# One transformer block on one core: the opening, the planner's rules for small runs, and two transpositions

## The chip, the cores and the metric

The kernel runs on one core of a Trainium2 chip. The metric is device time in microseconds (us) of one execution; lower is better. All engines run their own in-order instruction lists and wait for each other by semaphores: TensorE (PE in the rows, PEld for its weight loads), VectorE (DVE), ScalarE (ACT), GpSimd (POOL), and SyncE (SP), which issues most DMAs.

## The reference

One block for 256 tokens of width 2048, all in float32: a feed-forward (width 5632) added with weight 0.5, a mixer, and a second feed-forward, each between two RMS norms.

```python
def _rmsnorm(x, g):
    return x * rsqrt(mean(x * x, axis=-1) + 1e-6) * g
def _swiglu(x, w_gate, w_up, w_down):
    return (silu(x @ w_gate) * (x @ w_up)) @ w_down

h = x
f = _swiglu(_rmsnorm(h, ln_ffn1_pre), ffn1_gate, ffn1_up, ffn1_down)
h = h + 0.5 * _rmsnorm(f, ln_ffn1_post)
u = _rmsnorm(h, ln_mix_pre)
z_a, z_b, g_a, g_b = split(u @ w_in)              # 3360, 1024, 2048, 2048 columns
y_a = _rwkv7_branch(z_a, ...) @ w_proj_a          # a recurrence over the 256 tokens, 16 heads of 64
y_b = _pool_branch(z_b, ...) @ w_proj_b           # means over windows of 2, 4, 8, 16 tokens
h = h + _rmsnorm((sigmoid(g_a) * y_a + sigmoid(g_b) * y_b) @ w_out, ln_mix_post)
f = _swiglu(_rmsnorm(h, ln_ffn2_pre), ffn2_gate, ffn2_up, ffn2_down)
out = h + 0.5 * _rmsnorm(f, ln_ffn2_post)
```

## The kernel before

**Products.** A matrix product runs on TensorE in three matmuls per tile: each float32 operand is split into a rounded part (H, made by ScalarE as a copy to fp32r) and the rest (L, made by VectorE as a difference), and `mm3` adds H x H, H x L and L x H into a PSUM bank. Tokens are taken in two halves of 128, the inner dimension in k-tiles of 128, the columns in blocks of 512. Weights come by DMA in loads of two k-tiles (512 KB) into five buffers `w32`, and are split into five pairs `wH`, `wL`.

**Quads.** `Columns` makes two column blocks (f and l: gate and up, or two blocks of a down projection) at once. A pair of k-tiles that is a "quad" is done with seven products in place of eight, by sums of the operands (`sums`, names sf, sH, sL) and sums of the weights (names t, t13, t4), which VectorE makes. `GATE_QUADS` says how many quads each of the eleven blocks of a feed-forward has. In `block_seq` the first four products of a quad (`early`) run within the block before, the other three (`late`) within its own. The down projections use `quad` (all seven products at once); `OUT_QUADS` says for w_out how many quads there are, behind how many pairs the first comes, and how many pairs lie between them. Pairs that are quads are left out of the list `rest`, so with two quads w_out begins with k-tiles 4 and up.

**Transposed activations.** A product needs its activations with the inner dimension on the partitions. There are two ways. `transpose_split`: TensorE transposes four 128x128 tiles into a bank (tile names tr, zT, rb, pr), and the split reads the bank. `turn` and `carry`: VectorE transposes 32x32 blocks within T1 (name T), SP writes it to DRAM (name cx) and reads it back in four pieces (name x) in the wanted order, and the split reads that. The feed-forwards' hidden blocks go the second way; the norms' results and the mixer's mixed output mT go the first.

**Opening.** `head` turns 12 identity tiles (name warm), while x and the first gate column arrive; x is turned by TensorE, scaled by the gains `g1` (from a 16-row load g1rows, turned by TensorE as pg) and split; with each turned tile ScalarE sums the squares of x (name junk). Then come the 16 k-tiles of the gate column. The small parameter rows (cols) of the mixer are loaded later on SP's queue and turned by TensorE as the pair pr.

**End of a stage.** `post` evaluates the norm behind a product: for its last column block `ev` sums squares on ScalarE (junk), scales by the gains on VectorE (fg), makes the root on GpSimd (rs), and adds the residual.

**Mixer.** `MIX_ORDER` lists its products. The recurrence runs in two halves of eight heads (`rwkv`); its matmuls are small (names pA, pB, pM, pX, pU, pSa, pS, pY), use part of TensorE's rows or columns, and form the stream "chain". The results yH, yL go through w_proj_a: `pairs` does columns 0 and 1 together, k-tiles 0 to 3 of both, then 4 to 7; `gemm_tok` does columns 2 and 3 one by one. `ev_pa` multiplies by the gate sga, adds mb, and transposes into mT, which w_out reads.

**Planner.** No order is written by hand. `Plan.add` records every operation with its costs; `deadlines` works out due times, and `simulate` runs a model of the engines with a clock of its own and emits the operations in the order in which they start there. On TensorE the streams have ranks: chain, side (transpositions), main. Chain operations with the same array shape form a run (`o.run`); a run starts when `whole` finds the inputs and banks of its first 16 operations ready, and once begun goes on as its operations come free, with main matmuls in between where one is not. Two engines do not read one bank at a time (`i.lock`).

Of the kernel before, what the change touches and what calls it, by code (L numbers as in the profile page):

```python
# [19 lines left out]
P = 128  # L20
# [20 lines left out]
WARM = 12  # L41
# [4 lines left out]
GATE_QUADS = [0, 0] + [3, 4] * 4 + [3]  # L46
OUT_QUADS = ((2, 2, 1.0), (2, 1, 1.0))
# [3 lines left out]
HOLD = 3e5  # L51
Z_DMA = "k0 v0 k1 v1 r1"
# [14 lines left out]
class TileInfo:  # L67
    __slots__ = ("tag", "left", "slot", "seq", "writes", "reads", "psum", "dl", "home", "lock")
# [15 lines left out]
RUN = 16  # L84
TABLES = {AF.Exp: (0,), AF.Sigmoid: (2,), AF.Tanh: (0, 2, 18), AF.Silu: (18,)}
# [3 lines left out]
class Plan:  # L89

    def __init__(s, tc):
# [5 lines left out]
        s.clk, s.stream, s.lag, s.dl0 = 0.0, "main", 12000.0, None  # L97
# [13 lines left out]
    def tile(s, shape, dt, tag, name, pool, bufs):  # L111
        s.tags[tag] = bufs
        t = s.track(s.shadow.dram_tensor(name, tuple(shape), dt).ap(), tag)
        s.tiles[name].home = pool, list(shape), dt
        return t
# [34 lines left out]
    def add(s, eng, name, fn, a, k):  # L150
# [11 lines left out]
        s.cost(o, name, w, r, k)  # L162
        seen = set()
# [77 lines left out]
    def deadlines(s):  # L241
# [9 lines left out]
        for o in s.ops:  # L251
# [8 lines left out]
            if not run or run[-1].cfg != o.cfg or far >= idx[run[0].i]:  # L260
                run = []
# [12 lines left out]
    def simulate(s):  # L274
# [38 lines left out]
        def whole(o):  # L313
            if o.run is None or o.run is held:
                return True
            for x in o.run[:RUN]:
# [4 lines left out]
            need = {id(i) for x in o.run[:RUN] for i in x.psum if i.slot is None}  # L321
            return len(need) <= len(slots["pt"])

        def go(o):
# [144 lines left out]
class Block:  # L469
# [105 lines left out]
    def mm3(s, ps, aH, aL, bH, bL, start, stop, **k):  # L575
# [3 lines left out]
        nc.tensor.matmul(ps, aL, bH, start=False, stop=stop, **k)  # L579

    def gemm_tok(s, w, c0, at, KT, evac, lead=False, trail=False, xs=None, cw=512):
# [3 lines left out]
        def do(k, h):  # L585
            (wH, wL), (xH, xL) = ws[k], at(k)
            s.mm3(pss[h][:, :cw], xH[:, h * P:h * P + P], xL[:, h * P:h * P + P], wH, wL,
                  k == 0, k == KT - 1)
# [64 lines left out]
    def head(s, w, c0, KT, do, keep, xs):  # L653
        load, turn = xs
# [51 lines left out]
    def transpose_split(s, src, T, j, h, gT=None, stream="side"):  # L706
        nc = s.nc
        with s.set(stream=stream):
            ps = s.psum("tr").rearrange("p (k t) -> p k t", k=4)
            for i in range(4):  # L710
                nc.tensor.transpose(ps[:, i], src[:, i * P:(i + 1) * P], s.ident)
        dH = T[j][0][:, :, h * P:h * P + P]
        dL = T[j][1][:, :, h * P:h * P + P]
        if gT is not None:
# [7 lines left out]
            return  # L722
# [22 lines left out]
    def carry(s, T1, T):  # L745
        v = s.carry_raw(T1)
        T.extend(s.new_T(1))
        for h in range(2):
            H, L = [t.rearrange("p k (h i t) -> p k h i t", h=2, i=4)[:, :, h] for t in T[-1]]
# [1128 lines left out]
```

## Time and profile before

| | |
|---|---|
| median of 3 runs | 2022.7 us (2022.35 to 2023.87) |
| the profiled execution | 2022.16 us |
| its span in the trace | 2020.2 us |
| TensorE busy | 2002.1 us (99%), 9835 matmuls |
| VectorE busy | 1750.4 us (87%) |
| ScalarE busy | 1185.9 us (59%) |
| GpSimd busy | 80.7 us (4%) |
| DMA | 469.87 MB, mean 233 GB/s |
| granted TensorE clock | 0.999 |

Times in rows are us from the start of the span. A row of a timeline has its start, its length, the engine, the line of the kernel (a helper's, so it is the same for most), the operation, out<-in by the program's names, the shape and the count; in brackets the idle time of the engine before it and what ended it. Matmuls overlap in the pipeline, so a row's length is more than its share of TensorE's time; from start to start is the better measure. A row of the waits has who waited for whom, us in total, times, and the longest.

### The profile page before, as it was taken

The page shows a single profiled execution, that of the slowest core. Times are in us where ns is not written, and L with a number is a line of the kernel's source. Part 1 is how long each engine was busy: PE and PEld are TensorE (multiplying, and loading weights), DVE is VectorE, ACT ScalarE, POOL GpSimd, SP SyncE. Part 2 cuts the span into 40 slices and gives each one's busy share as a digit, 9 for nine tenths or more (in the row PEclk, how much of TensorE's full clock was granted, in tenths as well). Part 3 has the DMA queues.
Part 4 walks back from the last instruction along what each step waited for, and adds up shares of the span by engine and source line. Part 5 has one row for each costly group of instructions (what it writes and reads, how often), then busy time and mean ns, then how long its engine had stood idle before and what let it go on. Part 6 is the DMA issues. An engine that isn't in the chain of part 4 may idle for free.

```text
span 2020.2 us, 28152 instructions
## 1 busy us (share of the span) xinstructions
PE 2002.1 (99%) x9835; PEld 1652.7 (82%) x9835; DVE 1750.4 (87%) x2284; ACT 1185.9 (59%) x1592; POOL 80.7 (4%) x148
## 2 busy tenths in 40 slices
PE   9999999999999999999999999999999999999998
PEld 7888888888888888887888788888888888788886
DVE  8999999999988758897868779798999999898885
ACT  7555656565555556764846455575555665655552
POOL 0000000000001110001200110010000000000000
PEclk9999999999999999999999999999999999999999
DMA  7788888886667677756475475667888888876673
GB/s 266 239 261 268 281 268 275 266 282 219 214 203 258 214 249 206 221 162 209 143 233 179 145 261 197 200 209 241 273 273 276 269 270 273 280 227 203 208 253 133
DMA packets 254054, 469.87 MB, mean 233 GB/s; under 512 B 20559, under 2 KB 42201, under 8 KB 253913
## 3 DMA queue, kind: packets, MB, share of 16 engines
q1 hardware_dynamic: 247737, 447.63, 68.5%
q0 software_dynamic: 5888, 19.93, 2.8%
q8 instruction: 77, 1.26, 0.3%
q14 instruction: 64, 0.52, 0.1%
q10 hardware_dynamic: 288, 0.52, 0.1%
HBM read 444.40 MB, written 23.59 MB: 232 GB/s over the span
## 4 chain that ended last, share of the span: by engine, by line
PE 79%; DVE 9%; DMA 6%; issue 3%; ACT 2%; SPq 1%; DVEq 0%; ACTq 0%; POOLq 0%
PE l L455 26%; PE f L455 23%; PE mm L455 22%; PE p L455 5%; DVE wL L455 4%; DMA w<-in_ffn_gate_dram 2%; DMA x<-cx 2%; DVE t L455 1%; ACT wH L455 1%; SPq L455 1%; DMA w<-in_ffn_up_dram 1%; PE tr L455 1%; DVE w L455 0%; PE pY L455 0%; DMA x<-in_x_dram 0%
## 5 line engine op out<-in xcount | busy, mean ns | idle before, releaser
L455 ACT CAST wH<-w 128x1024 fp32r<-128x1024 f32 (+2 forms) x722 | 746.7, 1046 | 632.4 <-DVE w L455 170.8
L455 DVE TENSOR_TENSOR wL<-w,wH 128x1024 fp32r<-128x1024 f32 (+2 forms) x722 | 863.2, 1210 | 167.6 <-ACT wH L455 163.4
L455 PE MATMUL l<-wL,xH 128*128 128x512 f32 x784 | 305.7, 390 | 0.8 <-DVE wL L455 0.7
L455 PE MATMUL l<-wH,xH 128*128 128x512 f32 x784 | 305.4, 390 | 0.0
L455 PE MATMUL l<-wH,xL 128*128 128x512 f32 x784 | 305.3, 389 | 0.0
L455 PE MATMUL mm<-wL,xH 128*128 128x512 f32 (+1 forms) x672 | 261.6, 389 | 0.0
L455 PE MATMUL mm<-wH,xH 128*128 128x512 f32 (+1 forms) x672 | 261.1, 389 | 0.0
L455 PE MATMUL mm<-wH,xL 128*128 128x512 f32 (+1 forms) x672 | 260.7, 388 | 0.0
L455 PE MATMUL f<-wH,xH 128*128 128x512 f32 x664 | 258.5, 389 | 0.0
L455 PE MATMUL f<-wL,xH 128*128 128x512 f32 x664 | 258.4, 389 | 0.0
L455 PE MATMUL f<-wH,xL 128*128 128x512 f32 x664 | 258.4, 389 | 0.0
L455 DVE TENSOR_TENSOR t<-w,w 128x1024 f32<-128x1024 f32 (+1 forms) x160 | 162.1, 1013 | 14.6 <-DMA w<-in_ffn_down_dram 8.0
L455 PEld LDWEIGHTS l<-wL,xH 128*128 128x128 f32 x784 | 147.2, 188 | 32.5 <-DVE wL L455 2.2
L455 PEld LDWEIGHTS l<-wH,xH 128*128 128x128 f32 x784 | 147.2, 188 | 30.6
L455 PEld LDWEIGHTS l<-wH,xL 128*128 128x128 f32 x784 | 147.2, 188 | 30.1
L455 PEld LDWEIGHTS mm<-wL,xH 128*128 128x128 f32 x672 | 126.4, 188 | 25.2 <-DVE wL L455 0.4
L455 PEld LDWEIGHTS mm<-wH,xH 128*128 128x128 f32 x672 | 126.3, 188 | 24.9
L455 PEld LDWEIGHTS mm<-wH,xL 128*128 128x128 f32 x672 | 126.2, 188 | 24.8 <-DVE xL L455 0.4
L455 PEld LDWEIGHTS f<-wH,xH 128*128 128x128 f32 x664 | 124.6, 188 | 26.0
L455 PEld LDWEIGHTS f<-wL,xH 128*128 128x128 f32 x664 | 124.6, 188 | 25.9
L455 PEld LDWEIGHTS f<-wH,xL 128*128 128x128 f32 x664 | 124.6, 188 | 25.8
L455 DVE TENSOR_TENSOR wL<-t,wH 128x1024 fp32r<-128x1024 f32 x98 | 119.0, 1214 | 3.0 <-ACT wH L455 2.8
(307 smaller groups left out, 2697.4 us busy)
## 6 DMA issues: line engine op xcount, KB each, us to landing
w<-in_w_in_dram SPq DMA_DIRECT2D x128, 512.0 KB
w<-in_ffn_up_dram SPq DMA_DIRECT2D x114, 512.0 KB
w<-in_ffn_gate_dram SPq DMA_DIRECT2D x112, 512.0 KB
w<-in_ffn_down_dram SPq DMA_DIRECT2D x112, 512.0 KB
w<-in_ffn_gate_dram SPq DMA_DIRECT2D x190, 256.0 KB
w<-in_ffn_up_dram SPq DMA_DIRECT2D x186, 256.0 KB
w<-in_ffn_down_dram SPq DMA_DIRECT2D x128, 256.0 KB
cx<-T SPq DMA_DIRECT2D x29, 512.0 KB
```

The costliest lines, as they stand in the source:

```text
L455: ins = o.fn(*[real(x) for x in o.a], **{n: real(x) for n, x in o.k.items()})
```

## The change

- `head`: the row of gains is loaded first (with a due time far ahead) and turned before x; 16 identity turns before and 8 more behind the turn of the first two tiles of x, in a bank of the other kind; the squares of x are no longer summed with each turn but all behind k-tile 11 (`SQ`).
- `GATE_QUADS`: block 3 (the third entry) has 2 quads, not 3, in both feed-forwards.
- The planner counts TensorE's first 4.8 us of its clock double (`COLD`). Runs are cut at 16 operations and where the kind of bank changes, and `whole` asks for all of a run. In a small array shape, TensorE is left idle when the next run of the chain is ready within 400 ns (`soon`, `STAY`).
- `behind`: an operation can be put behind another in the plan. In `post`, the scaling of the last column block is put behind the step that follows its square sum.
- `ev_pa`: the blocks 0 and 1 of mT go by `turn` and `carry`; `pairs` is no longer used, and the four columns of w_proj_a run one by one. The first quad of w_out comes behind 3 pairs, not 2.

```diff
-WARM = 12
+WARM = 16
+WARM2 = 8
-GATE_QUADS = [0, 0] + [3, 4] * 4 + [3]
-OUT_QUADS = ((2, 2, 1.0), (2, 1, 1.0))
+GATE_QUADS = [0, 0, 2, 4, 3, 4, 3, 4, 3, 4, 3]
+OUT_QUADS = ((2, 3, 1.0), (2, 1, 1.0))
+MIX_DMA = 2
+COLD = 4800.0
+SQ = 11
+STAY = 400.0
...
# Plan.add
+        if s.behind is not None:
+            o.preds.add(s.behind.i)
...
# Plan.deadlines
-            if not run or run[-1].cfg != o.cfg or far >= idx[run[0].i]:
+            if not run or run[-1].cfg != o.cfg or far >= idx[run[0].i] or len(run) == RUN \
+                    or run[-1].psum[0].kind != o.psum[0].kind:
                 run = []
...
# Plan.simulate
-            for x in o.run[:RUN]:
+            for x in o.run:
...
+        def soon(o):
+            for x in o.run or [o]:
+                for q in x.preds:
+                    y = ops[q]
+                    if y.eng != "PE" and (y.start is None or y.end + 305.0 > now + STAY):
+                        return False
+            need = {id(i) for x in o.run or [o] for i in x.psum if i.slot is None}
+            return len(need) <= len(slots["pt"])
...
+            if e == "PE" and now < COLD:
+                pace, dur = 2 * pace, dur + pace
...
+                            if q and st == "chain" and cfg != (0, 0) and can(q[0]) and soon(q[0]):
+                                break
...
# head
-        ps = s.psum("warm")
+        ps = s.bank("warm")
         for _ in range(WARM):
             s.nc.tensor.transpose(ps[:, :P], s.ident, s.ident)
+        load(None, None)
         load(0, 0)
         load(1, 0)
-        load(None, None)
...
-        turn(1, 0)
+        last = turn(1, 0)
         split(2)
         split(3)
+        with s.set(behind=last):
+            for _ in range(WARM2):
+                s.nc.tensor.transpose(ps[:, :P], s.ident, s.ident)
         for k in range(KT):
             do(k, 0)
-            do(k, 1)
+            last = do(k, 1)
...
+            if k == SQ:
+                late = last
+        with s.set(behind=late):
+            for c in range(4):
+                for h in range(2):
+                    square(h, c)
...
# post, last column block
                     s.sumsq(ps, ss[h][:, c:c + 1])
-                    norm(h, r)
-                    scale()
+                    with s.set(behind=norm(h, r)):
+                        scale()
...
# mixer, ev_pa
-                s.transpose_split(sg, mT, c, h)
+                if c >= MIX_DMA:
+                    s.transpose_split(sg, mT, c, h)
+                    return
+                if not h:
+                    T1.append(s.unit(p="T1"))
+                s.turn(T1[0], h, sg)
+                if h:
+                    s.carry(T1[0], mT, c)
...
-        s.pairs(prm["w_proj_a"], (0, 512), at_a, NKW, 4, (ev_pa(0), ev_pa(1)))
-        for c in range(2, 4):
+        for c in range(4):
             s.gemm_tok(prm["w_proj_a"], c * 512, at_a, NKW, ev_pa(c))
...
# tile_block_kernel, load(None, None)
-                nc.sync.dma_start(out=gr, in_=ln_ffn1_pre[0].rearrange("(k p) -> k p", p=P))
+                with s.set(lag=-20000.0):
+                    nc.sync.dma_start(out=gr, in_=ln_ffn1_pre[0].rearrange("(k p) -> k p", p=P))
```

More of the change, by code (lines that the diff above doesn't have):

```diff
@@ L67 @@
 class TileInfo:
-    __slots__ = ("tag", "left", "slot", "seq", "writes", "reads", "psum", "dl", "home", "lock")
+    __slots__ = ("tag", "left", "slot", "seq", "writes", "reads", "psum", "dl", "home", "lock", "kind")
 class Engine:
@@ L114, in tile @@
         s.tiles[name].home = pool, list(shape), dt
+        s.tiles[name].kind = name.rsplit("_", 1)[0]
         return t
@@ L578, in mm3 @@
         nc.tensor.matmul(ps, aH, bL, start=False, stop=False, **k)
-        nc.tensor.matmul(ps, aL, bH, start=False, stop=stop, **k)
+        return nc.tensor.matmul(ps, aL, bH, start=False, stop=stop, **k)
     def gemm_tok(s, w, c0, at, KT, evac, lead=False, trail=False, xs=None, cw=512):
@@ L653, in head @@
     def head(s, w, c0, KT, do, keep, xs):
-        load, turn = xs
+        load, turn, square = xs
         w32 = {}
@@ L710, in transpose_split @@
             for i in range(4):
-                nc.tensor.transpose(ps[:, i], src[:, i * P:(i + 1) * P], s.ident)
+                last = nc.tensor.transpose(ps[:, i], src[:, i * P:(i + 1) * P], s.ident)
         dH = T[j][0][:, :, h * P:h * P + P]
@@ L1111, in emit @@
                     s.rstd(ss[h], D, rs[h])
-        return uT, rs, emit
+        def emit(h, c, ap):
+            s.transpose_split(ap, uT, c, h, gT())
+            square(h, c, ap)
+        return uT, rs, emit, square
     def tok(s, w, c0, at, KT, evac):
@@ L1373, in ev_pa @@
         def ev_pa(c):
+            T1 = []
             def ev(h, ps):
@@ L1795 @@
         g1 = s.const([P, 16], "g1")
-        uT, rs, pre = s.next_pre(lambda: g1)
+        uT, rs, _, square = s.next_pre(lambda: g1)
         nc = s.nc
```

35 lines of the change are left out of this document (19 added, 16 removed).

## The prediction

> **What bounds the kernel now.** I read the page first, then the waits of TensorE, then the chain of waits, then the timeline at the places that the change touches: the opening, the small matmuls of the recurrence, the end of the mixer, the end of the kernel.
>
> ```profile
> span 2020.2 us, 28152 instructions
> ...
> PE 2002.1 (99%) x9835; PEld 1652.7 (82%) x9835; DVE 1750.4 (87%) x2284; ACT 1185.9 (59%) x1592; POOL 80.7 (4%) x148
> ```
>
> TensorE (PE) is busy 2002.1 of 2020.2 us. The time is therefore the length of its instruction list, plus its few waits, plus what lies before its first and after its last instruction. An edit pays if it shortens that list or one of these waits, and an edit that relieves VectorE (87%) or ScalarE (59%) pays only through a wait of TensorE. From the waits of TensorE, the three that the change could reach outside the recurrence (total us, times, longest):
>
> ```profile
> PE l L455 <- DVE hL L455: 1.5, 2, 1.2
> PE pr L455 <- DMA cols<-in_pool_scale_dram: 1.2, 1, 1.2
> ...
> PE l L455 <- DVE wL L455: 0.7, 1, 0.7
> ```
>
> The profiled execution took 2022.16 us, 2.0 more than its span; the median of the three runs is 2022.7, 0.54 above it. The sum below is made against 2022.16, and 0.54 is added at its end. About 0.2% (4.05 us) is what a measurement of this kernel tells from no change.
>
> **Part 1: one quad less in each feed-forward.** The third entry of GATE_QUADS goes from 3 to 2. A quad does seven products (four in `early`, three in `late`) where plain pairs of k-tiles do eight (2 k-tiles, 2 halves, 2 columns); a product is three matmuls. From the chain of waits, start, us and what:
>
> ```profile
> 1259.87 16.32 PE l L455 x72
> ```
>
> 16.32 / 72 = 0.227 us per matmul back to back. So 3 x 0.227 = 0.68 us more in each of the two feed-forwards, **+1.36 us**, all on TensorE. VectorE is relieved of a quad's additions and splits; at most this ends the waits for hL and wL shown above (2.2 us), but the trace has those waits in later blocks, so I count nothing; the range keeps both ends.
>
> **Part 2: two blocks of the mixer's output by VectorE.** For columns 0 and 1 the four groups of four transpositions leave TensorE. The timeline shows two such groups between matmuls:
>
> ```profile
> 1204.77 0.60 PE L455 MATMUL tr<-ident,sga 128*128 128x128 f32 x4
> 1205.12 0.48 PE L455 MATMUL mm<-wH,yL 128*128 128x512 f32 x1
> 1205.45 0.60 PE L455 MATMUL tr<-ident,sga 128*128 128x128 f32 x4
> ...
> 1206.12 0.39 PE L455 MATMUL mm<-wL,yH 128*128 128x512 f32 x1
> ```
>
> From 1204.77 to 1206.12 are 1.35 us with two matmuls of 0.227 in them, so 0.90 for two groups, 0.45 each (the slower matmul behind a group included). Four groups: **-1.79 us**. What they cost elsewhere must be hidden: VectorE's transposition, a write to DRAM, four reads, the splits. The same route is in the feed-forward, and the rows around the mixer's end give the room:
>
> ```profile
> 57.56 1.29 DVE L455 STREAM_TRANSPOSE T<-sg 128x512 f32<-128x512 f32 x2
> ...
> 69.38 1.14 ACT L455 CAST xH<-x 128x512 fp32r<-128x512 f32 x2 [0.84 <-DMA x<-cx]
> ```
> ```profile
> 1184.20 0.68 DVE L455 TENSOR_TENSOR yL<-qb,yH 128x512 fp32r<-128x512 f32 x1
> ...
> 1186.63 0.39 PE L455 MATMUL mm<-wH,yH 128*128 128x512 f32 x1
> ...
> 1232.94 0.39 PE L455 MATMUL f<-wH,xH 128*128 128x512 f32 x1
> ```
>
> The product with w_proj_a begins at 1186.63. A column is 8 k-tiles x 2 halves x 3 matmuls x 0.227 = 10.9 us, so column 1 ends at 1208.4 when the columns run one after the other. VectorE then has four operations on 128x512 (0.68 each by the yL row) and 1.29 of transposition, 4.0 us; from there to the first split of the landed tile pass 10.5 us (58.85 to 69.38), and splitting takes some 2.5: ready near 1225.4. w_out starts with k-tiles 4 to 7, which are column 1, near 1231 (1186.63 + 43.5 + 0.9 of remaining groups). Some 5.6 us to spare, so nothing is added. The new DMAs go on SP's queue between the loads of w_out; what is queued behind them are those loads. The first quad of w_out moves one pair later (OUT_QUADS), which gives column 0 time and changes no count: 0. Without `pairs`, k-tile 4 of the first column is needed at 1186.63 + 24 x 0.227 = 1192.1, before it was 5.4 us later; yL is done at 1184.9. 7.2 us to spare: 0.
>
> A rule of the Trainium skill speaks against this part: VectorE: DVE Perf Modes, Rules for kernel authors, says to transpose a full 128x128 on TensorE if PSUM is an acceptable destination. By it the four groups stay and the sum would be 1.79 us higher. I keep the rows, because TensorE is the engine with no idle time here and VectorE has some.
>
> **Part 3: last square first.** At the very end:
>
> ```profile
> 2011.14 0.69 DVE L455 TENSOR_TENSOR fg<-l,gb 128x512 f32<-128x512 f32 x1 [5.74 <-PE l L455]
> 2011.87 0.60 ACT L455 ACTIVATE junk<-l 128x512 bf16<-128x512 f32 x1 [10.19 <-DVE fg L455]
> ...
> 2012.59 0.21 DVE L455 TENSOR_SCALAR rt<-ss,rp 128x1 f32<-128x1 f32 x1 [0.75 <-ACT junk L455]
> ...
> 2013.53 2.74 DVE L455 SCALAR_TENSOR_TENSOR fg<-fg,rs,h 128x512 f32<-128x512 f32 x4 [0.73 <-POOL rs L455]
> ```
>
> The square waits 0.73 us for the scaling. With `behind` the square comes first and the scaling runs while GpSimd takes the power: 0.73 us of VectorE's idle time before 2013.53 holds its 0.69. Nothing else is late there: **-0.73 us**. At the ends of the first feed-forward and the mixer TensorE has other matmuls: 0.
>
> **Part 4: the opening.** TensorE's first rows, VectorE's first two and ScalarE's first scaled one:
>
> ```profile
> 1.71 2.82 PE L455 MATMUL warm<-ident 128*128 128x128 f32 x12 [1.71 <-POOL ident masks.py:199]
> 5.28 1.97 PE L455 MATMUL tr<-ident,x 128*128 128x128 f32 x8 [0.75 <-DMA x<-in_x_dram]
> 7.18 0.28 PE L455 MATMUL pg<-ident,g1rows 16*128 16x16 f32 x1
> ...
> 8.17 0.78 PE L455 MATMUL mm<-wH,xH 128*128 128x512 f32 x1
> ...
> 28.34 0.39 PE L455 MATMUL mm<-wL,xH 128*128 128x512 f32 x1
> 29.95 0.53 PE L455 MATMUL pr<-ident,cols 128*128 128x128 f32 x2 [1.22 <-DMA cols<-in_pool_scale_dram]
> ```
> ```profile
> 6.52 0.69 DVE L455 TENSOR_TENSOR wL<-w,wH 128x512 fp32r<-128x512 f32 x1 [6.52 <-ACT wH L455]
> 7.50 0.17 DVE L455 COPY g<-pg 128x16 f32<-128x16 f32 x1 [0.29 <-PE pg L455]
> ```
> ```profile
> 7.71 0.88 ACT L455 ACTIVATE xH<-tr,g 128x128 fp32r<-128x128 f32 x3
> ```
>
> The first product waits for the gains (7.18, 7.50, 7.71, then 8.17), although x is turned and the first weights are split by 7.21. With the row first, about 1 us of this goes. But the stretch ends at 29.95, where TensorE waits 1.22 us for small rows queued behind x (2 MB), the gate's first column (4 MB) and five loads of the up column (2.5 MB); those transfers do not change. A faster opening alone only lengthens that wait. The gain is the number of matmuls that the planner places ahead of the pr pair: it puts the pair where its own clock has the rows landed, and its matmuls begin earlier by about the 0.7 us that pass from 7.50 to 8.17, so 3 more come first: **-0.68 us**. Bounds: 0 and -1.22. The eight extra turns cost 8 x 2.82 / 12 = 1.9 us ahead of the first product at worst, most of it in idle time; up to 0.54 (1.22 - 0.68) more is covered by the same wait. The squares, moved from between the turns to behind k-tile 11, lie on ScalarE; what waits for them are rs, the Silu and the sums for the next quads, which `GATE_QUADS` also asks for later: 0.
>
> **Part 5: whole runs.** In the recurrence a run of pA and pB is now at most 16 operations of one kind of bank, and starts when all of it can. Now they are broken up (first half), while the first pA goes through whole:
>
> ```profile
> 866.73 0.39 PE L455 MATMUL mm<-wH,xH 128*128 128x512 f32 x1
> 867.05 2.05 PE L455 MATMUL pA<-AR,BK 64*128 64x128 f32 x32
> 869.04 0.50 PE L455 MATMUL mm<-wL,xH 128*128 128x512 f32 x1
> ...
> 882.10 0.24 PE L455 MATMUL pB<-ident,BK 64*128 64x64 f32 x1 [0.30 <-ACT X L455]
> 882.27 0.51 PE L455 MATMUL mm<-wH,xL 128*128 128x512 f32 x1
> 882.71 0.70 PE L455 MATMUL pB<-ident,BK 64*128 64x64 f32 x15
> ...
> 888.51 0.39 PE L455 MATMUL mm<-wL,xH 128*128 128x512 f32 x1
> 888.83 0.72 PE L455 MATMUL pB<-ident,BK 64*128 64x64 f32 x16
> 889.48 0.50 PE L455 MATMUL mm<-wH,xL 128*128 128x512 f32 x1
> ```
>
> A whole pA costs 869.04 - 866.73 - 0.23 = 2.08 us, a whole pB 889.48 - 888.51 - 0.23 = 0.74, and the matmul behind each takes 0.11 more than usual (0.50 against 0.39). The stretches by window, large matmuls (mm) alone; one of each count began before and one at the end:
>
> ```profile
> 881.41:889.48 8.07, 3.55 (x12) 1.00 0.54 165
> 1077.89:1084.13 6.24, 2.83 (x10) 1.00 0.01 3
> ```
>
> First half: 8.07 - 10 x 0.227 = 5.80 for two pB and one pA, which whole would be 2 x 0.74 + 2.08 + 0.22 = 3.78: 2.0 too many. Second half: 6.24 - 8 x 0.227 = 4.42 for one pB and one pA, whole 0.74 + 2.08 + 0.11 = 2.93: 1.5. Of these 3.5 us about 1 is waiting on ScalarE and VectorE, which can come back; I take **-2.8 us**, bounds 0 and -3.5. STAY lets TensorE idle up to 400 ns in place of going back to large matmuls; no row shows it, and I take 0 between -0.5 and +0.5.
>
> Sum: 1.36 - 1.79 - 0.73 - 0.68 - 2.80 = -4.64. 2022.16 - 4.64 = 2017.5, and 0.54 more is **2018.0 us**.
>
> **The rivals.** (a) The gains of parts 4 and 5 do not come: the pr pair keeps its place, and the runs, which the planner cuts by its estimates, still break on the chip's real waits. Then 2018.0 + 0.7 + 2.8 = 2021.5. For it: the breaks have waits in them (0.30 before 882.10). Against it: the rule acts on the order itself. (b) The plan is redrawn everywhere, and the waits for hL and wL (2.2 us) and the rest of the pr wait (0.5) go too: 2015.3. For it: they are single waits with no pattern. Against it: nothing in the change is aimed at them. (c) Slower: a whole run waits for all its banks, so the recurrence ends later, and w_proj_a's k-tile 4 now comes earlier. Place: the second half, before 1192.1. From a delay of 7.2 us on, each us is one of TensorE's waiting, since w_proj_a is next in its order. In the first half pB began 13 us after pA had ended (869.04 to 882.10); a hold of that size for both pB and the second pA would end the recurrence some 17 us later, a wait of 10: 2028. Against it: the matmuls that fill the hold exist, and yL has its 7.2 us. (d) The rule of the skill holds: the route takes twice its 10.5 us beside w_out's loads, column 1 is ready at 1235.9, 4.9 after 1231, so 2022.9.
>
> **How the numbers follow.** Forecast 0.57, (a) 0.17, (b) 0.13, (c) 0.08, (d) 0.05. The forecast's own range is 2016.2 (part 4 at -1.22, part 5 at -3.5, STAY at -0.5) to 2020.3 (half of part 5, 0.4 of part 4 lost, STAY at +0.5); 0.40 of its 0.57 I put beyond 4.05 us (below 2018.65) and 0.17 within. Faster: 0.40 + 0.13 = 0.53. Same: 0.17 + 0.17 + 0.05 = 0.39. Slower: 0.08. The range 2014.8 to 2022.3 takes in the forecast, (a) and nearly all of (b).
>
> **What would show it.** Right: TensorE's matmul count six large ones higher; transpositions of sga x16 instead of x32, with two more writes of cx and eight more reads; junk ahead of fg at the end and the last gap 0.7 shorter; pB in groups of 16 and pA of 32; the wait of pr about half as long. Wrong: a wait of f or mm for xL or yL after 1186, pr's wait longer than 1.2, or new waits of l for wL in the first 140 us, which would mean that late squares starve the sums.

## The result and the profile after

The changed kernel takes 2033.3 us (median of 10 runs, 2028.6 to 2038.7) where the kernel before, on the same chip, takes 2022.7 (10 runs, 2021.0 to 2026.2): a ratio of 1.0052, 95% interval 1.0040 to 1.0064, so 10.5 us slower. Forecast were 2018.0 us and a range of 2014.8 to 2022.3; the time lies 11 us above the range. The profiled execution took 2032.80 us, its span is 2031.1. All readings below are of profiled executions; differences between kernels that were measured in runs are given as ratios to the kernel before, which ran beside them each time (its median there was 2023.8 to 2025.0); a thousandth of the ratio is 2.0 us. The code stands on other lines now: what was L455 is L477 in the changed kernel, and between L455 and L479 in the others.

The page of the changed kernel, and the waits of its TensorE (total us, times, longest):

```profile
span 2031.1 us, 28147 instructions
...
PE 2002.6 (99%) x9837; PEld 1655.5 (82%) x9837; DVE 1744.9 (86%) x2278; ACT 1185.6 (58%) x1588; POOL 80.9 (4%) x148
```
```profile
PE tr L477 <- DVE sga L477: 8.5, 1, 8.5
PE pS L477 <- ACT Z L477: 2.9, 1, 2.9
...
PE tr L477 <- DMA x<-in_x_dram: 1.7, 1, 1.7
PE l L477 <- DVE hL L477: 1.4, 2, 1.2
PE pk L477 <- DVE nb L477: 1.2, 1, 1.2
...
PE pr L477 <- DMA cols<-in_pool_scale_dram: 0.5, 1, 0.5
```

TensorE is as busy as before (2002.6 against 2002.1 us). It has two matmuls more than before: six large ones more by part 1, twelve more turns of the identity by part 4, and sixteen transpositions fewer by part 2. The span grew by 10.9, and one line carries most of it: a transposition of sga waits 8.5 us for VectorE, a wait that the kernel before does not have. Its place in the timelines of TensorE, ScalarE, VectorE and GpSimd (start, us, what, and in brackets the idle time before it and who ended it):

```profile
1223.57 0.39 PE L477 MATMUL mm<-wH,yL 128*128 128x512 f32 x1
1232.42 1.09 PE L477 MATMUL tr<-ident,sga 128*128 128x128 f32 x4 [8.47 <-DVE sga L477]
1233.16 0.78 PE L477 MATMUL mm<-wH,yH 128*128 128x512 f32 x1
...
1236.29 0.63 PE L477 MATMUL mm<-wH,yL 128*128 128x512 f32 x1
...
1237.11 0.39 PE L477 MATMUL mm<-wL,yH 128*128 128x512 f32 x1
```
```profile
1214.52 1.05 ACT L477 CAST wH<-w 128x1024 fp32r<-128x1024 f32 x1 [2.39 <-DMA w<-in_w_proj_a_dram]
1223.53 1.14 ACT L477 CAST xH<-x 128x512 fp32r<-128x512 f32 x2 [7.96 <-DMA x<-cx]
1224.58 2.93 ACT L477 CAST wH<-w 128x1024 fp32r<-128x1024 f32 x3
```
```profile
1202.15 1.30 DVE L477 STREAM_TRANSPOSE T<-sga 128x512 f32<-128x512 f32 x2
...
1224.18 1.29 DVE L477 TENSOR_TENSOR xL<-x,xH 128x512 fp32r<-128x512 f32 x2 [8.80 <-ACT xH L477]
1225.40 2.35 DVE L477 TENSOR_TENSOR wL<-w,wH 128x1024 fp32r<-128x1024 f32 x2
...
1230.40 1.28 DVE L477 TENSOR_TENSOR sga<-mm,sga 128x512 f32<-128x512 f32 x2
```
```profile
1189.68 0.53 POOL L477 DMA_DIRECT2D h<-hsp  x1 [11.80 <-PE mm L477]
1202.64 0.53 POOL L477 DMA_DIRECT2D h<-hsp  x1 [12.42 <-DVE sga L477]
1203.85 0.53 POOL L477 DMA_DIRECT2D h<-hsp  x1 [0.69 <-DVE T L477]
1209.56 0.53 POOL L477 DMA_DIRECT2D h<-hsp  x1 [5.18 <-ACT wH L477]
```

Read from the end: TensorE's transposition of column 2 needs sga, which VectorE makes at 1230.40. It makes it late because it stood idle for 8.80 us, up to 1224.18, waiting for xH. ScalarE made that late because it stood idle for 7.96 us, up to 1223.53, waiting for column 0 to come back through cx. Nothing on TensorE needs column 0 then. But each engine works its list off in order, and the split of column 0 stands in both lists ahead of the weight casts and of column 2's evacuation. Column 0 had been transposed at 1203.45, so 20.1 us passed up to the split, where the feed-forward's route, by the prediction's rows, takes 10.5. In these 20 us three of the four loads of h and one of gb (512 KB each, issued by GpSimd) run beside the write and the reads of cx and the weight loads: between 1203 and 1224 GpSimd's queue moves 2.10 MB and SP's 3.83. The time goes into the reads and not into the write. They are issued by 1211.16, and 12.4 us pass from there to the split:

```profile
1208.99 2.17 SPq L477 DMA_DIRECT2D x<-cx  x4
```

The wait has a sequel. Busy time of TensorE and its granted clock (PEclk) in stretches of 4 us:

```profile
core 0: us, PE busy (x), PEclk, DMA share, GB/s
1224.00:1228.00 4.00, 0.00 (x0) 0.85 0.31 116
1228.00:1232.00 4.00, 0.00 (x0) 0.50 0.87 255
1232.00:1236.00 4.00, 3.58 (x13) 0.50 0.98 291
1236.00:1240.00 4.00, 4.00 (x17) 0.87 0.45 143
```

The clock falls to half during the wait and stays there until about 1237: from 1233.16 to 1237.11 pass 3.95 us with seven large matmuls and a group of transpositions, which at the prediction's durations take 7 x 0.227 + 0.45 = 2.04. With the slow group at 1232.42 that is some 2.2 us more. The Trainium skill, TensorE: Matmul & The Clock Gate, What's actually happening, says that an idle window of about 3.4 us halves the clock and about 3.4 us of sustained work restore it; by that rule a wait of 8.5 us is followed by slow matmuls, and the trace agrees.

The whole difference by position: counting all matmuls of 256 columns and more, number 5132 starts at 1223.31 us before and 1222.89 after (0.4 earlier), number 5142 at 1226.14 and 1236.72: 11.0 us are lost between them. The last one starts 11.7 us later, of which six more products are 1.36; the end of the kernel behind it takes 8.64 in place of 9.52.

### The profile page after: what moved, and what is told of

Its sections match the earlier page's. It is cut to its first block, busy times and chain, and to the rows that moved or that the text cites. A ratio compares the mean times of both kernels' runs of the same rounds, so it can differ in the third digit from the quotient of the medians.

```text
span 2031.1 us, 28147 instructions
## 1 busy us (share of the span) xinstructions
PE 2002.6 (99%) x9837; PEld 1655.5 (82%) x9837; DVE 1744.9 (86%) x2278; ACT 1185.6 (58%) x1588; POOL 80.9 (4%) x148
## 4 chain that ended last, share of the span: by engine, by line
PE 68%; DVE 13%; DMA 8%; issue 5%; ACT 4%; SPq 1%; DVEq 0%; POOL 0%; ACTq 0%; POOLq 0%
PE l L477 23%; PE f L477 20%; PE mm L477 18%; DVE wL L477 6%; PE p L477 5%; DMA x<-cx 3%; DMA w<-in_ffn_gate_dram 3%; ACT wH L477 2%; DVE t L477 2%; SPq L477 1%; DMA w<-in_ffn_up_dram 1%; DVE w L477 1%; DMA w<-in_w_proj_a_dram 1%; DVE T L477 1%; PE tr L477 0%
## 5 line engine op out<-in xcount | busy, mean ns | idle before, releaser
L477 ACT CAST wH<-w 128x1024 fp32r<-128x1024 f32 (+2 forms) x722 | 748.2, 1047 | 625.9 <-PE mm L477 142.8
L477 DVE TENSOR_TENSOR wL<-w,wH 128x1024 fp32r<-128x1024 f32 (+2 forms) x722 | 864.6, 1211 | 162.3 <-ACT wH L477 158.5
L477 PE MATMUL l<-wL,xH 128*128 128x512 f32 x788 | 307.1, 390 | 0.0
L477 PE MATMUL l<-wH,xH 128*128 128x512 f32 x788 | 306.9, 389 | 0.0
L477 PE MATMUL l<-wH,xL 128*128 128x512 f32 x788 | 306.6, 389 | 0.0
L477 PE MATMUL f<-wL,xH 128*128 128x512 f32 x672 | 261.7, 389 | 0.2 <-DVE wL L477 0.2
L477 PE MATMUL f<-wH,xL 128*128 128x512 f32 x672 | 261.6, 389 | 0.0
L477 PE MATMUL f<-wH,xH 128*128 128x512 f32 x672 | 261.4, 389 | 0.0
L477 PE MATMUL mm<-wH,xH 128*128 128x512 f32 (+1 forms) x672 | 261.0, 388 | 0.0
L477 PE MATMUL mm<-wH,xL 128*128 128x512 f32 (+1 forms) x672 | 260.9, 388 | 0.0
L477 PE MATMUL mm<-wL,xH 128*128 128x512 f32 (+1 forms) x672 | 260.6, 388 | 0.1
L477 PEld LDWEIGHTS l<-wL,xH 128*128 128x128 f32 x788 | 147.9, 188 | 31.5 <-DVE wL L477 0.7
L477 PEld LDWEIGHTS l<-wH,xH 128*128 128x128 f32 x788 | 147.9, 188 | 30.6
L477 PEld LDWEIGHTS l<-wH,xL 128*128 128x128 f32 x788 | 147.9, 188 | 30.2
L477 DVE TENSOR_TENSOR t<-w,w 128x1024 f32<-128x1024 f32 (+1 forms) x156 | 158.5, 1016 | 16.1 <-DMA w<-in_ffn_down_dram 8.3
L477 PEld LDWEIGHTS f<-wL,xH 128*128 128x128 f32 x672 | 126.1, 188 | 27.0 <-DVE wL L477 0.7
L477 PEld LDWEIGHTS f<-wH,xH 128*128 128x128 f32 x672 | 126.2, 188 | 26.1
L477 PEld LDWEIGHTS f<-wH,xL 128*128 128x128 f32 x672 | 126.2, 188 | 26.1
L477 PEld LDWEIGHTS mm<-wH,xL 128*128 128x128 f32 x672 | 126.2, 188 | 25.0
L477 PEld LDWEIGHTS mm<-wL,xH 128*128 128x128 f32 x672 | 126.2, 188 | 25.0 <-DVE wL L477 0.5
L477 PEld LDWEIGHTS mm<-wH,xH 128*128 128x128 f32 x672 | 126.2, 188 | 24.5
L477 DVE TENSOR_TENSOR wL<-t,wH 128x1024 fp32r<-128x1024 f32 x96 | 116.8, 1217 | 5.5 <-ACT wH L477 5.1
```

The source lines that it names most:

```text
L477: ins = o.fn(*[real(x) for x in o.a], **{n: real(x) for n, x in o.k.items()})
```

## The experiments

**Four runs on the wait: without the route, the route alone, later splits, later reloads.**

```diff
# e1_no_route, against the changed kernel
-MIX_DMA = 2
+MIX_DMA = 0
```

> The changed kernel with MIX_DMA = 0: all four columns of the mixer's output are transposed by TensorE again, the rest of the change stays. Theory (the route makes the wait of 8.5 us for sga at the end of the mixer, and the slow matmuls behind it): the wait and the slow matmuls (2.2 us) go and four groups of four transpositions come back (+1.8), so 2033.3 - 8.5 - 2.2 + 1.8 = 2024.4 us. Rival (the wait is the doing of the new order of the recurrence, and only shows at this place): a wait of over 4 us stays near 1223 and the time stays above 2030. If moreover the opening and the whole runs bring what the prediction gave them, the time is 2018.0 + 1.8 = 2019.8.

Measured: 2024.02 us, 0.9995 of before (0.9983 to 1.0007). The list of TensorE's waits has none for sga any more, and the clock stays at 1.00 from 1224 to 1240. The reloads by GpSimd are early again, the last of the four before 1191:

```profile
1185.22 0.53 POOL L477 DMA_DIRECT2D h<-hsp  x1 [7.37 <-ACT wH L477]
1188.17 0.53 POOL L477 DMA_DIRECT2D h<-hsp  x1 [2.43 <-DVE qb L477]
1189.42 1.12 POOL L477 DMA_DIRECT2D h<-hsp  x2 [0.72 <-PE mm L477]
```

So part 2 carries the whole loss, and parts 1, 3, 4 and 5 together bring about 1 us (by the interval, from 3.4 us gained to 1.4 lost) where the prediction had 2.85.

```diff
# e2_route_only, against the kernel before
-OUT_QUADS = ((2, 2, 1.0), (2, 1, 1.0))
+OUT_QUADS = ((2, 3, 1.0), (2, 1, 1.0))
+MIX_DMA = 2
...  # carry(s, T1, T, j=None) and ev_pa as in the change
-        s.pairs(prm["w_proj_a"], (0, 512), at_a, NKW, 4, (ev_pa(0), ev_pa(1)))
-        for c in range(2, 4):
+        for c in range(4):
```

> The kernel before with part 2 alone: MIX_DMA = 2, the four columns of w_proj_a one after the other, and the first quad of w_out one pair later. Theory (the route alone is enough): a wait of 6 to 9 us for sga near 1225 and slow matmuls behind it, 2022.7 - 1.8 + 8.5 + 2.2 = 2031.6 us. Rival (it takes the new order of the recurrence too, which delays the tiles that the reloads wait for): no wait over 2 us there, 2022.7 - 1.8 = 2020.9.

Measured: 2036.57 us, 1.0053 of before (1.0034 to 1.0072). The route alone is enough:

```profile
PE tr L456 <- DVE sga L456: 9.0, 1, 9.0
```

The h loads are issued at 1187.88, 1201.01, 1202.22 and 1207.36, as in the changed kernel, so it is the route that moves them: its tiles T1 and x32 come from the same 34 units as h, and the loads wait for units that the route holds or that come free later (the second and third row of GpSimd above wait for sga and for T). That the units are the reason is read from these rows; no run gave the route units of its own.

```diff
# e3_late_split, against the changed kernel
-                o.end = dma + LAND
+                o.end = dma + LAND + o.far
...
-                    s.carry(T1[0], mT, c)
+                    with s.set(far=5000.0):
+                        s.carry(T1[0], mT, c)
```

> The changed kernel in which the planner counts 5 us more for each of the two steps (write, read back) of the two mixer blocks, so that their splits stand behind more weight casts in the lists of ScalarE and VectorE; no instruction is added. Theory (the splits stand too early in lists that are worked off in order, and what waits for them is the work behind them): the wait for sga falls below 2 us, and with it the slow matmuls; 2033.3 - 8.5 - 2.2 = 2022.6 us or a little more. Rival (the blocks themselves come too late for w_out, or the weights of w_out do): a wait of mm for xL, xH, wH or wL of 4 us or more takes its place, and the time stays above 2029.

Measured: 2029.32 us, 1.0020 of before (1.0011 to 1.0029). TensorE's waits at the place:

```profile
1239.78 1.48 PE L479 MATMUL tr<-ident,sga 128*128 128x128 f32 x8 [2.72 <-DVE sga L479]
...
1242.58 0.80 PE L479 MATMUL f<-wH,xH 128*128 128x512 f32 x1 [1.31 <-ACT xH L479]
...
1244.20 0.80 PE L479 MATMUL f<-wH,xL 128*128 128x512 f32 x1 [0.40 <-DVE xL L479]
```

Neither side comes out in full: the wait for sga is 2.7 us and not under 2, and the rival's time comes (above 2029) without its wait of 4 us. Moving the splits behind more of the casts takes 5.8 us off the first wait, so the order of the lists does carry the price. But the transfer is as slow as ever (22.4 us from the end of the transposition at 1206.80 to the split at 1229.21, still with 2.46 us of idle ScalarE ahead of it), and now w_out does wait for a block, 1.7 us, at half clock. Order alone cannot mend a transfer that takes twice its time.

```diff
# e4_reload_late, against the changed kernel
+        o.sem = s.behind if o.nbytes else None
...
+                if o.sem is not None:   # a real wait, not only one in the plan
+                    s.tc.add_manual_dep(ins.ins, did[o.sem.i].ins.name, info, reason="slot")
...
                 if h == 0:
-                    reload()
+                    with s.set(behind=s.last):   # the last transposition of sga by TensorE
+                        reload()
```

> The changed kernel with the four loads of h from hsp (2 MB, by GpSimd) held until the last transposition of the mixer's output by TensorE, so that they no longer lie in the same time as the write and the reads of cx. Theory A (they compete with the transfers of cx for the DMA engines): from the transposition of column 0 to its split passes 12 us or less in place of 20, the wait for sga falls below 2 us, 2033.3 - 10.7 = 2022.6 us. Theory B (the queue of weight loads on SP alone makes the transfer that slow): 17 us or more, and a wait of 5 us or more stays: above 2028.

Measured: 2022.50 us, 0.9985 of before (0.9975 to 0.9995): some 13.6 us faster than the changed kernel by the two ratios, with the same work, and faster than the kernel before.

```profile
1238.55 2.25 POOL L478 DMA_DIRECT2D h<-hsp  x4 [60.36 <-PE f L478]
```
```profile
1215.91 1.14 ACT L478 CAST xH<-x 128x512 fp32r<-128x512 f32 x2 [0.75 <-DMA x<-cx]
```
```profile
1208.74 1.84 SPq L478 DMA_DIRECT2D x<-cx  x4
```

With the loads of h held until 1238.55 (and with them the load of gb, which stands behind them in GpSimd's list), column 0 is transposed at 1203.76 (end) and split at 1215.91: 12.2 us in place of 20.1, at the edge of what theory A asked for. From the end of the issue of the reads (1210.58) to the split pass 5.3 us in place of 12.4, so 7 of the 8 us are lost in the reads; from the issue of the write to that of the reads it is 4.9 (from 1203.84) in place of 5.5 (from 1203.53). ScalarE waits 0.75 for it, TensorE 0.5 for sga, and its clock stays at 1.00. So the wait of 8.5 us rests on two things, the transfer slowed by GpSimd's loads and a split that stands early in lists worked off in order; taking the first away leaves 0.5 us of it, taking the second away 2.7. The Trainium skill, DMA: Bandwidth & Descriptors, Issuing engines are not separate DMA queues, says that transfers issued by GpSimd and by SP run on the same 16 DMA engines and interleave; the trace agrees, since loads on another engine's queue lengthen SP's round trip from 12.2 to 20.1 us.

**The other parts alone.** Four runs on whole runs (part 5) and on the quad (part 1), all but the first on top of the held reloads:

```diff
# e5_runs_only, against the kernel before: part 5 alone
-            if not run or run[-1].cfg != o.cfg or far >= idx[run[0].i]:
+            if not run or run[-1].cfg != o.cfg or far >= idx[run[0].i] or len(run) == RUN \
+                    or run[-1].psum[0].kind != o.psum[0].kind:
...  # whole over the run, soon and STAY as in the change
```

> The kernel before with part 5 alone (runs of one kind of bank, at most 16, started whole, and STAY). Theory P (the prediction's step): broken runs become whole at no other cost, -2.8 us, a ratio to before of 0.9986. Theory N (read from the profiles with part 5, which all show a wait of pk for nb of 1.2 us and mostly a wait of pS for Z of over 2.5, where those without it show 0 and 0.9 to 1.4): the runs become whole, and these two waits, some 3 us, take the gain back; a ratio of 1.000 within 0.001, and both waits in the profile. If the two waits are missing here, they come from another part.

```diff
# e6_late_old_quads, against e4_reload_late
-GATE_QUADS = [0, 0, 2, 4, 3, 4, 3, 4, 3, 4, 3]
+GATE_QUADS = [0, 0] + [3, 4] * 4 + [3]
# e7_late_no_runs, against e4_reload_late: the lines of e5 undone
# e8_late_no_runs_old_quads: both
```

> The kernel with the held reloads (e4_reload_late) with GATE_QUADS as before the change: one quad more in each feed-forward. By the count of matmuls (6 x 0.227) it is 1.36 us faster than that one: 0.9985 - 0.0007 = 0.9978 of before. Rival (the quad left out relieved VectorE of waits that come back): waits of l for hL and wL of over 1.4 us more in the sum, and no gain, 0.9985 or more.

> The kernel with the held reloads (e4_reload_late) without part 5, so with the rule of before for runs. Theory P: 2.8 us slower than that one, 0.9999 of before. Theory N: no slower than 0.5 us, perhaps 1 faster, 0.998 to 0.9988; the wait of pk for nb is gone and that of pS for Z is under 1.5.

> Both at once: held reloads, GATE_QUADS and the rule for runs as before the change; what stays of the change is the route, the last square and the opening. By sums: -1.8 (route) - 0.75 (square) - 0.1 (opening, as the profiles show it) = -2.65 us against before, a ratio of 0.9987. With theory N the one with the old quads and part 5 comes out alike, within 0.7 us; with theory P that one is 2.8 faster.

Measured: e5 2025.70 us, 1.0002 of before (0.9991 to 1.0012); e6 2023.86 us, 0.9995 (0.9985 to 1.0005); e7 2022.18 us, 0.9985 (0.9977 to 0.9994); e8 2025.33 us, 1.0000 (0.9990 to 1.0011). Part 5 brings nothing that can be measured, alone (e5) or beside the rest (e7 against e4): theory N, except that the wait of pS is not its doing, since e7 without it still has 2.5 us. With the old quads the kernel is slower, not faster, by 2.0 us (e6 against e4) and 3.0 (e8 against e7) by the ratios, each uncertain by almost 3 us as worked out from the two intervals: the sum that predicted -1.36 seems to have missed an interaction, which the next runs look for.

**The opening and the quad.**

```diff
# e9_head_only, against the kernel before: part 4 alone (head, load, square and COLD as in the change)
# e10_head_and_quads, against e9_head_only
-GATE_QUADS = [0, 0] + [3, 4] * 4 + [3]
+GATE_QUADS = [0, 0, 2, 4, 3, 4, 3, 4, 3, 4, 3]
# e11_quad_first_only, against e7_late_no_runs
-                              su, [2 * i for i in range(GATE_QUADS[b])],
+                              su, [2 * i for i in range(GATE_QUADS[b] + (b == 2 and xs is None))],
# e12_no_head, against e8_late_no_runs_old_quads: the opening as in the kernel before
```

> The kernel before with part 4 alone (row of gains first, more turns of the identity, square sums from k-tile 11). Prediction's step: -0.68 us, a ratio of 0.9997. Theory S (read from e6 and e8, where the late squares put the Silu of block 0 some 3 us later and the sums of the first quads with it): the pr pair stays at 30.0 to 30.1 with one matmul more ahead, and a wait of l for wH and wL of 1.3 to 1.6 us appears near 79; +1.3 us, a ratio of 1.0006.

> The kernel before with parts 4 and 1 (the opening, and 2 quads in block 3). Theory S: the wait near 79 is gone, since there is a quad less to prepare, and six matmuls more come instead, +1.36 - 0.1: a ratio of 1.0006, the same as with part 4 alone within 1 us. Rival (the quad left out relieves more than this wait, as the medians of e4 against e6 and of e7 against e8 would have it, 2.0 and 3.1 us): 0.9995 or less, faster than part 4 alone by 2 us or more.

> The kernel with held reloads and without part 5 (e7_late_no_runs) with the quad left out in the first feed-forward alone; the second has its three quads in block 3 again. Theory S (the quad left out pays only where the late squares are): 3 matmuls less, -0.68 us, 0.9982 of before. Rival (it relieves VectorE in both): not faster than e7_late_no_runs, 0.9985 or more, and waits of l for hL or wL of over 0.7 near 1390.

> What the other runs leave as paying, alone: the kernel before with the route of part 2, the last square first, and the reloads held; opening, quads and runs as before the change. By sums: -1.8 - 0.75 + 0.5 (wait for sga that the held reloads leave) = -2.0 us, 0.9990. With theory S it is 1.3 us or more faster than e8_late_no_runs_old_quads, which has the new opening too (1.0000).

Measured: e9 2027.83 us, 1.0018 (1.0009 to 1.0026); e10 2025.91 us, 1.0006 (0.9997 to 1.0015); e11 2022.89 us, 0.9989 (0.9980 to 0.9998); e12 2023.74 us, 0.9994 (0.9984 to 1.0004). Part 4 alone costs 3.6 us, more than theory S has. Its wait near 79 us, on TensorE, and on ScalarE the Silu of block 0 that stands at its root (e9, and below it the same Silu in a kernel with the early squares, e13_quads_only):

```profile
78.52 0.39 PE L463 MATMUL f<-wH,xL 128*128 128x512 f32 x1
79.60 0.50 PE L463 MATMUL l<-wH,xH 128*128 128x512 f32 x1 [0.70 <-ACT wH L463]
80.86 0.50 PE L463 MATMUL l<-wL,xH 128*128 128x512 f32 x1 [0.76 <-DVE wL L463]
```
```profile
39.68 1.27 ACT L463 ACTIVATE sg<-mm,rs 128x512 f32<-128x512 f32 x2
```
```profile
35.97 0.69 ACT L455 ACTIVATE sg<-mm,rs 128x512 f32<-128x512 f32 x1
37.49 0.69 ACT L455 ACTIVATE sg<-mm,rs 128x512 f32<-128x512 f32 x1
```

The squares from k-tile 11 on put the scales rs, and with them the Silu, about 3 us later; what VectorE prepares for the quads moves with it, and TensorE waits 1.46 us. The same two waits are in e6 (1.3 us) and e8 (1.6 us), which have late squares and three quads, and, at this place, in no profile with two quads or with early squares. Two quads in block 3 leave VectorE the time: e10 has no such wait, and S's ratio, though it is 2.4 us faster than e9 where S had less than 1.

How much of this lies in the opening can be read by position. The 400th large matmul (512 columns) starts at 103.8 to 104.2 us in the seven profiles with the old opening, at 105.9 to 106.2 in the three with late squares and three quads, and at 104.3 to 104.7 in the seven with late squares and two. So the late squares cost about 2 us there; the quad left out takes back 1.5 of them, at a price of 0.68 for three more matmuls in each feed-forward, and 0.5 stays. The rest of e9's loss arises later.

e11 gives back the quad in the second feed-forward, where there are no late squares, and does not get the 0.68 us that theory S gives it (0.9989 against 0.9985; the intervals are wider than the difference, so this stays open).

**Part 1 alone, and without the opening.**

```diff
# e13_quads_only, against the kernel before
-GATE_QUADS = [0, 0] + [3, 4] * 4 + [3]
+GATE_QUADS = [0, 0, 2, 4, 3, 4, 3, 4, 3, 4, 3]
# e14_late_quads_no_head: e12_no_head with this line
# e15_late_quads_runs_no_head: e14 with part 5
```

> The kernel before with part 1 alone (2 quads in block 3 of each feed-forward). Prediction's step, and theory S (a quad less pays only where the late squares are): six matmuls more, +1.36 us, 1.0007. Rival R (it relieves VectorE of work by which TensorE waits in many places for hL and wL): 0.9993 or less, waits of l of 1.0 us or less in the sum, where the kernel before has 2.2.

> The kernel before with the route of part 2, held reloads, the last square first and part 1, so e7_late_no_runs (0.9985) with the opening of before. Theory S: e12_no_head + 1.36 us, 1.0001. Rival R: e12_no_head - 2 to 3 us, 0.9980 to 0.9984, and then faster than any kernel so far, if the opening costs anything.

> The same with part 5 as well, so the held reloads (e4_reload_late, 0.9985) with the opening of before: within 1 us of e14_late_quads_no_head, since part 5 by itself came out at 1.0002 and at no difference between e4 and e7. If the opening of part 4 costs 1 to 3 us, it is faster than e4_reload_late by that: 0.997 to 0.998.

Measured: e13 2026.76 us, 1.0012 (1.0003 to 1.0020); e14 2023.58 us, 0.9993 (0.9984 to 1.0002); e15 2021.95 us, 0.9994 (0.9985 to 1.0003). e13 is 2.4 us slower, with the sign of the prediction, and rival R's time does not come. But the profile does not put that loss where a quad is missing: e13 is 0.8 us behind the kernel before when the first feed-forward is done (first transposition of fg), 7.5 at the first product of w_proj_a and 6.2 at the end, so most of it arises in the mixer, which part 1 does not touch. R's other sign, waits of l of 1.0 us or less, does come (0.3), but these waits are between 0.2 and 4.4 us in the seventeen profiles, with two quads and with three, so it tells nothing. e14 lies between the two theories, and e15 does not reach the 0.997 to 0.998 expected of it.

By the ratios the opening, which alone costs 3.6 us, gains 1.2 to 1.8 where the quad is out (e10 against e13, e7 against e14, e4 against e15). Each of these differences is uncertain by some 2.5 us and taken from kernels on different chips, and at the 400th matmul the kernels with the new opening are 0.5 us later, not earlier. So that it gains there is not shown. What is shown of parts 1 and 4 together is the wait of 1.5 us that the one makes and the other takes away. The lowest ratios are those of e4_reload_late and e7_late_no_runs, both 0.9985 with intervals below 1: the first is the whole change with the reloads held, the second the same without part 5.

## Why the prediction was wrong, point by point

**Part 2, the step that failed.** "Some 5.6 us to spare, so nothing is added" was wrong in its time and in its victim. The time was the feed-forward's 10.5 us from transposition to split, taken over to a place where other loads run; it measured 20.1 (20.6 in e2, 22.4 in e3), and 12.2 with GpSimd's loads away. The prediction did look at the queue, but only at SP's ("what is queued behind them are those loads"); the loads that did the harm are GpSimd's, and the route brought them to this place (e1, e2), by our reading because it takes units that they need. The kernel before issues them between 1181.54 and 1186.98, over 16 us before the route's write (1203.53), so its trace had no row of the collision. The victim was taken to be w_out, which needs the blocks at 1231. It was column 2's evacuation, which needs no block at all and only stands behind the splits in the lists of VectorE and ScalarE. The question of who is queued behind the waiting instruction was put for SP and not for these two. Then the slow clock added some 2.2 us to 8.5, so the term that was put at nothing measured 10.7. The transpositions saved are real: from the first product of w_proj_a to the first of w_out pass 46.31 us in the kernel before and 44.47 in e7, which has the route and waits less than 0.2 us in this stretch; 1.84 less, against 1.79 in the sum.

Rival (d) came nearest, with 5 in 100: it had the transfer at twice its time, but let the loss begin only where w_out needs column 1, and so got 4.9 us. The rule of the Trainium skill to transpose on TensorE (VectorE: DVE Perf Modes, Rules for kernel authors) would have been the better choice for the change as it stands (by the two ratios e1 is some 11 us faster), but not for a reason in the transposition: VectorE's took 1.30 us for two, as in the feed-forward.

**Part 1** has its six matmuls, and e13 (+2.4, from 0.6 to 4.0) does not speak against their +1.36, though most of e13's loss lies elsewhere. It was wrong in being summed: with part 4's late squares it takes away a wait of 1.5 us.

**Part 3** was right. The end of the changed kernel, ScalarE and VectorE:

```profile
2022.83 0.60 ACT L477 ACTIVATE junk<-l 128x512 bf16<-128x512 f32 x1 [10.19 <-PE l L477]
```
```profile
2023.55 0.21 DVE L477 TENSOR_SCALAR rt<-ss,rp 128x1 f32<-128x1 f32 x1 [7.18 <-ACT junk L477]
2023.68 0.68 DVE L477 TENSOR_TENSOR fg<-l,gb 128x512 f32<-128x512 f32 x1
2024.49 2.74 DVE L477 SCALAR_TENSOR_TENSOR fg<-fg,rs,h 128x512 f32<-128x512 f32 x4
```

The square (junk) now comes ahead of fg, whose 0.68 lies in the time of GpSimd's power. From the start of the last matmul to the end of the span pass 8.64 us (9.52 before): 0.9 less, against 0.73. In the eleven profiles with part 3 it is 8.6 to 8.9 us, in the six without 9.4 to 10.1.

**Part 4** had the mechanism and missed the size and the price. The matmuls that were to begin 0.7 us earlier begin where x lands; the first product begins at 8.74 here, and at 7.4 to 8.3 in the other nine kernels with the new opening, against 8.17 before:

```profile
7.46 0.66 PE L477 MATMUL tr<-ident,x 128*128 128x128 f32 x4 [1.68 <-DMA x<-in_x_dram]
...
8.74 0.48 PE L477 MATMUL mm<-wH,xH 128*128 128x512 f32 x1
...
30.09 0.53 PE L477 MATMUL pr<-ident,cols 128*128 128x128 f32 x2 [0.55 <-DMA cols<-in_pool_scale_dram]
```

As foreseen, the pr pair holds the stretch (30.09, before 29.95), but one matmul more comes ahead of it and not three: the 101st large product starts at 35.3 to 35.6 us in ten profiles with the new opening and at 35.6 to 36.1 in seven with the old, 0.3 us on average against 0.68. The squares, counted at nothing because the quads were asked for later, cost about 2 us at the 400th matmul where the quad was not left out, 1.5 of them in the wait, and 0.5 where it was.

**Part 5** did what was said of the order and brought less. Runs of the recurrence in the changed kernel:

```profile
882.05 1.07 PE L477 MATMUL pB<-ident,BK 64*128 64x64 f32 x16
885.34 2.06 PE L477 MATMUL pA<-AR,BK 64*128 64x128 f32 x32
...
1076.45 2.05 PE L477 MATMUL pA<-AR,BK 64*128 64x128 f32 x30 [0.23 <-DVE AR L477]
...
1083.54 0.68 PE L477 MATMUL pB<-ident,BK 64*128 64x64 f32 x15 [0.30 <-DVE AR L477]
```

They start whole, in four pieces of each half, but then wait inside: the rule acts on the planner's estimate of when an operand is there. From the starts of the matmuls on both sides, the four runs of the first half cost 6.30 us in place of 7.64 and those of the second 7.10 in place of 7.24; with 0.11 for each matmul behind a break that is gone (two and two) that is 1.6 and 0.4 us, where 2.0 and 1.5 were said. And the wait of pk for nb, 1.2 us, is in all seven profiles with part 5 and in none of the ten without. What is left, 0.8 us, is less than the runs can tell (e5: -1.8 to +2.4). Rival (c) did not come: yL is done 5.2 us later than before (1190.09 against 1184.88), within the 7.2 to spare, and no product waits for it.

The sum, by what the runs show: part 2 +10.7 (e2, net of the transpositions saved, 6.9 to 14.6), parts 1 and 4 together +1.2 (e10), part 3 -0.9, part 5 about 0: +11.0, against the measured 10.5. The terms from runs are uncertain by 2 to 4 us each, so that the sum comes out this well is luck. In the profiles, 8.9 of the 10.8 us between the two spans arise between the first product of w_proj_a and the first of w_out (8.5 + 2.2 - 1.8).

## What to carry to other kernels

A round trip through DRAM has no price of its own: take its time from a row in which the same loads run beside it, and ask which transfers, of every issuing engine, the change itself will move into that time by taking their buffers. Where engines work lists off in order, an early place in a list makes a late operand everyone's wait: ask for each engine that handles it what stands behind, not only who needs the result. Edits that move work of one engine (late squares) and edits that relieve it (a quad less) are measured together as well as alone.

## What was not expected of the hardware

TensorE's clock also fell in waits far shorter than 8.5 us. The wait of pS for Z, near 950 us, is 0.9 us in the kernel before and between 1.3 and 3.5 in the sixteen others, with no pattern by part. Up to 1.4 us (three profiles) the clock stays at 1.00 behind it. From 2.0 to 3.5 us it falls to 0.50 in ten of fourteen, for 3.4 us in eight and 6.8 in two, and not in four (waits of 2.0, 2.1, 2.6 and 3.0). So the length of the wait alone does not decide, and by our estimate (half of the time at 0.50) such a wait may cost up to 1.7 or 3.4 us more than its own time. The Trainium skill, TensorE: Matmul & The Clock Gate, What's actually happening, has idle windows of about 3.4 us that run free of the kernel; here a wait of 2.0 us was enough.

Near 834 us the clock falls to 0.50 for 3.4 us in six profiles (e3, e8, e9, e12, e13, e14), in four of them with no wait of more than 0.2 us in the 8 us ahead. What stands there are sixteen very small matmuls. In e9 (the second row has the stretch, its length, TensorE's busy time and matmuls, its clock, the DMA share and GB/s):

```profile
831.72 1.95 PE L463 MATMUL pn<-bones,sq 128*128 128x2 f32 x16
```
```profile
834.00:836.00 2.00, 2.00 (x13) 0.60 0.03 11
```

TensorE is busy in all of this stretch, at a mean clock of 0.60. The other eleven profiles have the same sixteen matmuls and no fall. What decides stays open.

The falls also come and go between executions of one kernel: the kernel before has none near 834 or 950 in its profile, and its executions in the runs have mean clocks of 0.996 to 0.999, where one fall of 3.4 us takes 0.0008. So a difference of one or two us between two profiles may be such a fall. It is not the main part of the losses of e9 and e13: the executions of e9 have a mean clock of 0.9976 on average, those of the kernel before beside them 0.9981, and 0.0005 of 2025 us are 1.0 of its 3.6 us; for e13 it is 0.9978 against 0.9982, 0.8 of 2.4. Every change of the kernel's code redraws the order of the recurrence, and the wait of pS, the shortest in the kernel before, may hold another part; the runs do not separate it.
